# Layer norm and silu of a convolution in PSUM banks of their own, and silu's cast one tile later in ScalarE's order

## The chip, the cores and the metric

One core of a Trainium2 chip runs the kernel: TensorE (PE in the rows), VectorE (DVE), ScalarE (ACT), GpSimd (POOL), and SyncE (SP), which starts the loads and stores. The metric is the device time of one execution in microseconds, the median of the runs shown. Lower is better.

## The reference

A decoder layer on 512 tokens of width 1024, in float32. Two mixers work on the same normed input and are gated and added; an MLP with a squared ReLU follows. What matters here, cut down:

```python
u = rms_norm(x, norm_mix_g)
q, k, v, glu_in, gates = split(u @ w_in)
attn = sliding_window_attention(norm(q), norm(k), v, sinks, rel_bias) @ w_attn_o
a, gate = split(glu_in)
h = depthwise_conv(a * sigmoid(gate), w_dw, width=31) + b_dw
conv = silu(layer_norm(h, ln_g, ln_b)) @ w_conv_out
x = x + (sigmoid(gate_attn) * attn + sigmoid(gate_conv) * conv) @ w_out
x = x + square(relu(rms_norm(x, norm_mlp_g) @ w_ff1)) @ w_ff2
```

## The kernel before

**Tiling.** Activations stand transposed, 128 channels by 512 tokens to a tile; a projection to 1024 channels has eight such tiles. Every float32 product is made of three matmuls: each operand is split into a high part (rounded to fp32r, a cast on ScalarE) and a low part (the rest, a subtraction on GpSimd or VectorE), and high x high, high x low and low x high are added up in one PSUM bank. So a tile takes 8 x 3 = 24 matmuls of 512 columns.

**Stages.** First attention, the input projections and the 31 taps of the convolution (VectorE), side by side. Then the stage of the change: the attention output projection (`wo`, tiles ps_wo_0 to ps_wo_7), and beside it on the other engines the layer norm and silu of the eight convolution tiles; then the convolution output projection (`wc`, ps_wc), whose inputs are silu's high part sTh and low part sTl of all eight tiles; then w_out and the MLP in four parts, the second product of which keeps six banks in use at a time (ps_x, ps_y, ps_z, two each).

**Order.** Up to the end of `wc`, the order of the instructions on each engine is written out by hand: `at(position, function, arguments)` records an event, and the events are issued in the order of their positions (L992). One unit of position is six matmuls of a projection tile. Within an engine the order is strict; the engines wait for each other only through data and through buffers.

**Banks.** PSUM has eight banks. Two belong to the pool `aux`. The other six become the pool `psp` when attention closes (L830): one ring under the tag "mm". A tile asked for takes a bank of the ring, and if that bank's former tile still has readers, the first instruction that writes the new tile waits for them. In that ring stand the projection tiles, the mean (mu_ps), six squares (lsq) and eight silu values (y), in the order in which events ask for them.

**Layer norm.** `mean` (L854) makes the mean with two matmuls; `centre` (VectorE, L860) subtracts it; `square` (ScalarE, L868) squares, six of the tiles into PSUM; `square_sum` (VectorE, L876) adds them up in vsum; `var` (L880) sums over channels with sixteen small matmuls, takes 1/sigma on VectorE, and `spread` (L888) spreads it over the partitions with TensorE. Then per tile: `scale` (VectorE, L895), `silu_in` (ScalarE, L898: tanh into tz, then an affine y into PSUM), `silu` (VectorE, L905: y = (tz + 1) y), `silu_hi` (ScalarE, L909: the cast to sTh), `silu_lo` (VectorE, L912: sTl). On ScalarE stand between them the casts of the weight splits (L449), each followed by its low part on GpSimd (L452); SyncE's next load of weights waits for that low part. The evacuations of `wo` are on VectorE (L612), those of `wc` are three passes of VectorE and one of ScalarE (L614 to L619).

From w_out on, tiles are asked for in program order, again from `psp`.

Of the kernel before, what the change touches and what calls it, by code (L numbers as in the profile page):

```python
# [8 lines left out]
F32 = mybir.dt.float32  # L9
# [5 lines left out]
PSUM = bass.MemoryType.PSUM  # L15
DRAM = bass.MemoryType.DRAM

P = 128
S = 512
NT = 4  # L20
# [32 lines left out]
def tile_hybrid_block(  # L53
# [106 lines left out]
    def stationary_tiles(w, c0, n_tiles, name, lo_eng=None):  # L160

        for ch in range(n_tiles // 2):
            raw = wp.tile([P, KD, 256], F32, name=f"raw_{name}_{ch}", tag="raw", bufs=2)
            cols = slice(c0 + ch * 256, c0 + ch * 256 + 256)
            for kh in range(2):
                nc.sync.dma_start(
                    raw[:, 4 * kh:4 * kh + 4, :],
                    w[512 * kh:512 * kh + 512, cols].rearrange("(k p) c -> p k c", p=P),
                )
            for j in range(2):  # L170
                yield split(raw[:, :, j * P:(j + 1) * P], [P, KD, P], f"{name}_{ch}_{j}", lo_eng or ge)

    def moving_pieces(w, r0, nk, c0, width, name, lo_eng=None):

        kk = 1024 // width
        for ch in range(nk // (2 * kk)):
            raw = wp.tile([P, 2 * kk, width], F32, name=f"rawm_{name}_{ch}", tag="raw", bufs=2)
            for j in range(2):
                r = r0 + (ch * 2 + j) * kk * P
                nc.sync.dma_start(  # L180
                    raw[:, j * kk:(j + 1) * kk, :],
                    w[r:r + kk * P, c0:c0 + width].rearrange("(k p) c -> p k c", p=P),
                )
            for j in range(2):
                yield split(raw[:, j * kk:(j + 1) * kk, :], [P, kk, width], f"{name}_{ch}_{j}", lo_eng or ge)

    def mm_T(ps, wh, wl, ah, al, cols=slice(0, S), nk=KD):

        for k in range(nk):
            pe.matmul(ps, wh[:, k, :], ah[:, k, cols], start=(k == 0), stop=False)  # L190
            pe.matmul(ps, wh[:, k, :], al[:, k, cols], start=False, stop=False)  # L191
            pe.matmul(ps, wl[:, k, :], ah[:, k, cols], start=False, stop=(k == nk - 1))  # L192

    def mm_M(ps, ah, al, wh, wl, first, last):

        pe.matmul(ps, ah, wh, start=first, stop=False)  # L196
        pe.matmul(ps, ah, wl, start=False, stop=False)  # L197
        pe.matmul(ps, al, wh, start=False, stop=last)  # L198
# [144 lines left out]
    def at(pos, fn, *args):  # L343
        events.append((pos, len(events), fn, args))
# [109 lines left out]
    pool_of = {"mm": ps1}  # L454
# [178 lines left out]
    lnv = {}  # L633
# [168 lines left out]
    while any(left.values()):  # L802
# [3 lines left out]
        if live:  # L806
            ct = live[turn % len(live)]
# [19 lines left out]
    def close_attention():  # L827
        p1.close()
        pps.close()
        pool_of["mm"] = ctx.enter_context(tc.tile_pool(name="psp", bufs=6, space=PSUM, reuse_waits="tile"))  # L830
        lnv["pool"] = p2.enter_context(tc.tile_pool(name="ln", bufs=1, reuse_waits="tile"))
        aTh["t"] = lnv["pool"].tile([P, KD, S], F32R, name="aTh")
        lnv["sTh"] = lnv["pool"].tile([P, KD, S], F32R, name="sTh")
        lnv["sTl"] = lnv["pool"].tile([P, KD, S], F32R, name="sTl")
        lnv["vsum"] = [lnv["pool"].tile([P, S], F32, name=f"vsum{i}") for i in range(2)]
# [4 lines left out]
    def a_lo(g):  # L840
        if g == 0:
            aTh["l"] = keep.tile([P, KD, S], F32R, name="aTl", tag="act", bufs=2)
        ve.tensor_tensor(out=aTh["l"][:, 2 * g:2 * g + 2, :], in0=attnT[g],
                         in1=aTh["t"][:, 2 * g:2 * g + 2, :].bitcast(F32), op=ALU.subtract)

    at(END - 0.01, close_attention)
    for g in range(NG):
        at(END + 0.3 + g, a_hi, g)
        at(WO + 0.1 + 0.5 * g, a_lo, g)

    def lt(name):
        return lnv["pool"].tile([P, S], F32, name=name, tag="lt", bufs=4)
# [15 lines left out]
    def square(ct):  # L868
        vs = lnv["vsum"][ct % 2]
        if ct >= 6:  # L870
            se.activation(vs, cc[ct], AF.Square)
        else:
            sq = lnv["sq", ct] = pool_of["mm"].tile([P, S], F32, name=f"lsq_{ct}", tag="mm")
            se.activation(sq, cc[ct], AF.Square)

    def square_sum(ct):  # L876
# [20 lines left out]

    def silu_in(ct):  # L898
        tz = lt(f"tz_{ct}")
        y = pool_of["mm"].tile([P, S], F32, name=f"y_{ct}", tag="mm")  # L900
        lnv["y", ct] = (tz, y)
        se.activation(tz, cc[ct], AF.Tanh, scale=lnh[:, ct, 0:1], bias=lnh[:, ct, 1:2])
        se.activation(y, cc[ct], AF.Identity, scale=wcol[:, ct, CW + 1:CW + 2], bias=wcol[:, ct, CW + 2:CW + 3])
# [14 lines left out]
    for i, ct in enumerate((6, 7, 0, 1, 2, 3, 4, 5)):  # L918
        at(E + 1.3 + 0.5 * i, centre, ct)
        at(E + 1.7 + 0.5 * i, square, ct)  # L920
        if ct < 6:
            at(E + 2.8 + 0.5 * i, square_sum, ct)
    at(E + 8.5, var)
    at(E + 11.05, spread)
    for ct in range(KD):
        p = E + 11.1 + 1.35 * ct
        at(p, scale, ct)
        at(p + 0.5, silu_in, ct)
        at(p + 1.4, silu, ct)
        at(p + 1.7, silu_hi, ct)  # L930
        at(p + 2.75, silu_lo, ct)

    def merge_tiles():
        for n in "hl":
# [5 lines left out]
    with tc.manual_schedule(engines=START_ENGINES):  # L940
# [50 lines left out]
            pass  # L991
        for _, _, fn, args in sorted(events, key=lambda e: e[:2]):  # L992
            fn(*args)
    psp = pool_of["mm"]
    mTh, mTl = mT["h"], mT["l"]
    p2.close()
    gp.close()
# [20 lines left out]
    def mm_rows(accs, pieces, ah, al, kk):  # L1018

        n = len(pieces)  # L1020
        for i in range(n):
            for j in range(kk):
                for t in range(NT):
                    k = i * kk + j
                    mm_M(accs[t], ah(k, t), al(k, t), pieces[i][0][:, j, :], pieces[i][1][:, j, :], k == 0,
                         k == n * kk - 1)
# [3 lines left out]
    def residual(t, half, acc):  # L1030
        cols = slice(half * S, half * S + S)
        ve.tensor_tensor(out=x1[t][:, cols], in0=x1[t][:, cols], in1=acc, op=ALU.add)
        sq = row4k(f"fsq_{half}{t}")
        se.activation(sq[:, 0:S], x1[t][:, cols], AF.Square, accum_out=ssm[:, t, half:half + 1])

    def m_hi(k, t):
        return mTh[:, k, t * P:(t + 1) * P]

    def m_lo(k, t):
        return mTl[:, k, t * P:(t + 1) * P]  # L1040

    accs = [psp.tile([P, S], F32, name=f"ps_wo0_{t}", tag="mm") for t in range(NT)]
    mm_rows(accs, list(moving_pieces(w_out, 0, KD, 0, S, "wout0")), m_hi, m_lo, 2)
    for t in range(NT):
        residual(t, 0, accs[t])
# [11 lines left out]
    def x2_norm(t):  # L1057
        ms = sm.tile([P, 1], F32, name=f"ms_m{t}", tag="ms1")
        ve.tensor_tensor(out=ms, in0=ssm[:, t, 0:1], in1=ssm[:, t, 1:2], op=ALU.add)
        rs = rsqrt(mean_eps(ms, D, 1, f"m{t}"), 1, f"m{t}")  # L1060
        us[t] = row4k(f"u2_{t}")
        ve.scalar_tensor_tensor(out=us[t], in0=x1[t], scalar=rs, in1=gmlp, op0=ALU.mult, op1=ALU.mult)

    def x2_trans(t):
        transpose_split(aux, (us[t][:, 0:S], us[t][:, S:D]), x2Th, x2Tl, t, f"m{t}", "aux")

    for t in range(NT):
        acc = psp.tile([P, S], F32, name=f"ps_wo1_{t}", tag="mm")
        for k in range(KD):
            mm_M(acc, m_hi(k, t), m_lo(k, t), wout_h[k // 4][:, k % 4, :], wout_l[k // 4][:, k % 4, :],  # L1070
                 k == 0, k == KD - 1)
        residual(t, 1, acc)
        x2_norm(t)
        if t == 2:
            x2_trans(0)
# [31 lines left out]
    for part in range(PARTS):  # L1107
        tag = f"f{part}"
# [28 lines left out]

        early = []
        for m, (wh, wl) in enumerate(stationary_tiles(w_ff1, part * PT * P, PT, f"f1{part}", ve)):
            ps = psp.tile([P, S], F32, name=f"ps_f1{part}_{m}", tag="mm")  # L1140
            if part == 0 and m < EARLY:
                mm_T(ps[:, 0:256], wh, wl, x2Th, x2Tl, slice(0, 256))
                early.append((ps, wh, wl))
                if m < 2:
                    x2_trans(2 + m)
                if m == EARLY - 1:
                    for i, (ps_, wh_, wl_) in enumerate(early):
                        mm_T(ps_[:, 256:512], wh_, wl_, x2Th, x2Tl, slice(256, 512))
                        ff1_evac(ps_, i)
            else:  # L1150
                mm_T(ps, wh, wl, x2Th, x2Tl)
                ff1_evac(ps, m)
# [38 lines left out]
                    nc.sync.dma_start(out[n * P:(n + 1) * P, cols], x1[n][:, cols])  # L1191

        def two_banks(name):
            return [psp.tile([P, S], F32, name=f"ps_{name}{t}_{part}", tag="mm") for t in range(2)]

        def S_(i):
            return lambda t: a_of(aS, i, t)

        b11, b12, b22 = load(0, 0), load(0, 1), load(1, 1)
        X, Y = two_banks("x"), two_banks("y")  # L1200
        product(lambda t: a_of(aE, None, t), pieces_of(b11, f"b11_{part}"), X, True, True)
        add(0, 0, X, False)
# [58 lines left out]
```

## Time and profile before

| | us |
|---|---|
| median of 3 runs | 790.45 (789.98 to 791.97) |
| the profiled execution | 791.01 |
| its span, first to last instruction | 789.1 |
| TensorE busy in it | 775.8 |
| VectorE, ScalarE, GpSimd busy | 562.3, 404.8, 254.4 |

All times of rows are microseconds from the start of the span. A row of the timeline has the start, the duration, the engine, the line, the operation, what is written and from what, the shape, the count, and in brackets how long the engine stood idle before it and whom it waited for. Matmuls are pipelined: the distance from start to start counts, not the duration of one. [...]

### The profile page before, as it was taken

How to read it: one execution, taken by the hardware profiler on the slowest of the kernel's cores; microseconds unless marked ns; L12 is line 12 of the kernel's file. 1: busy time of each engine (PE TensorE's matmuls, PEld its weight loads, DVE VectorE, ACT ScalarE, POOL GpSimd, SP SyncE). 2: the span in 40 equal slices, each digit the busy share in tenths (PEclk: the TensorE clock that was granted, in tenths of full speed). 3: DMA queues.
4: the chain of work that ended last, by engine and by line, in shares of the span. 5: the costliest groups of instructions: out<-in, count | busy, mean ns of one | idle time of the engine just before them, and what ended most of it. 6: DMA issues, size and time to landing. Idle time of an engine off the chain costs nothing.

```text
span 789.1 us, 10436 instructions
## 1 busy us (share of the span) xinstructions
PE 775.8 (98%) x3960; PEld 658.2 (83%) x3960; DVE 562.3 (71%) x949; ACT 404.8 (51%) x683; POOL 254.4 (32%) x189
## 2 busy tenths in 40 slices
PE   8999999999999999998999999999999999999998
PEld 7989988898888888786888898888888888888886
DVE  5467978998888878966330886886678756875683
ACT  6445467676576655446233346443554365435640
POOL 4444978958565665423445000000000000000000
PEclk9999999999999999999999999999999999999999
DMA  7441041214141133422335344143224233331102
GB/s 255 139 154 54 3 158 54 92 43 134 53 135 54 56 105 102 166 69 91 107 107 155 100 149 157 54 159 103 68 97 148 69 105 108 107 106 54 36 19 106
DMA packets 64807, 79.56 MB, mean 101 GB/s; under 512 B 2980, under 2 KB 52180, under 8 KB 64758
## 3 DMA queue, kind: packets, MB, share of 16 engines
q1 hardware_dynamic: 64758, 78.91, 30.0%
q8 instruction: 31, 0.51, 0.3%
q14 instruction: 18, 0.15, 0.1%
HBM read 76.78 MB, written 2.12 MB: 100 GB/s over the span
## 4 chain that ended last, share of the span: by engine, by line
PE 89%; ACT 4%; DVE 3%; POOL 2%; DMA 1%; issue 1%; SPq 0%; DVEq 0%; ACTq 0%; POOLq 0%
PE ps_f L191 7%; PE ps_f L192 7%; PE ps_f L190 7%; PE ps_x L1181 4%; PE ps_x L1182 4%; PE ps_x L1179 4%; PE ps_ta L484 2%; PE ps_ta L486 2%; PE ps_g L484 2%; PE ps_ta L485 2%; PE ps_wo L198 2%; PE ps_wo L197 2%; PE ps_y L1181 2%; PE ps_y L1182 2%; PE ps_y L1179 2%; PE ps_wo L196 2%
## 5 line engine op out<-in xcount | busy, mean ns | idle before, releaser
L782 DVE SCALAR_TENSOR_TENSOR cv<-h,wcol,cv 128x512 f32<-128x512 f32 x208 | 147.5, 747 | 0.5
L191 PE MATMUL ps_f<-x2Tl,wh_f 128*128 128x512 f32 (+1 forms) x280 | 104.1, 372 | 0.1
L190 PE MATMUL ps_f<-x2Th,wh_f 128*128 128x512 f32 (+1 forms) x280 | 103.6, 371 | 0.2 <-ACT x2Th L208 0.2
L192 PE MATMUL ps_f<-x2Th,wl_f 128*128 128x512 f32 (+1 forms) x280 | 103.8, 371 | 0.0
L157 DVE TENSOR_TENSOR wl_f<-raw_f,wh_f 128x1024 fp32r<-128x1024 f32 x32 | 39.2, 1224 | 59.8 <-ACT wh_f L156 58.8
L156 ACT CAST wh_f<-raw_f 128x1024 fp32r<-128x1024 f32 x32 | 33.6, 1055 | 55.4 <-PE ps_f L191 36.9
L190 PEld LDWEIGHTS ps_f<-x2Th,wh_f 128*128 128x128 f32 x280 | 52.6, 188 | 9.6 <-ACT x2Th L208 0.5
L191 PEld LDWEIGHTS ps_f<-x2Tl,wh_f 128*128 128x128 f32 x280 | 52.7, 188 | 9.3 <-DVE x2Tl L209 0.3
L192 PEld LDWEIGHTS ps_f<-x2Th,wl_f 128*128 128x128 f32 x280 | 52.7, 188 | 9.0
L1102 ACT CAST wh_b<-b 128x1024 fp32r<-128x1024 f32 x24 | 25.3, 1056 | 40.5 <-PE ps_y L1182 13.1
L1089 DVE TENSOR_TENSOR wl_b<-b,wh_b 128x1024 fp32r<-128x1024 f32 x24 | 29.3, 1223 | 22.2 <-ACT wh_b L1102 22.2
L1102 ACT CAST wh_t<-t 128x1024 fp32r<-128x1024 f32 x24 | 24.9, 1054 | 35.5 <-DVE t L1089 15.6
L691 ACT ACTIVATE s<-s,negm 128x257 f32<-128x257 f32 (+1 forms) x64 | 30.4, 478 | 16.3 <-DVE negm L683 16.3
L196 PE MATMUL ps_q<-wh_q,uTh 128*128 128x256 f32 x128 | 36.6, 286 | 0.0
L198 PE MATMUL ps_q<-wh_q,uTl 128*128 128x256 f32 x128 | 36.2, 283 | 0.0
L197 PE MATMUL ps_q<-wl_q,uTh 128*128 128x256 f32 x128 | 36.2, 283 | 0.0
L715 DVE TENSOR_TENSOR pTl<-ptp,pTh 128x512 fp32r<-128x512 f32 x28 | 19.3, 691 | 23.4 <-ACT pTh L711 23.4
L774 POOL TENSOR_TENSOR side<-side,tap 128x512 f32<-128x512 f32 x24 | 31.2, 1299 | 13.6 <-ACT tap L773 13.6
L1089 DVE TENSOR_TENSOR wl_t<-t,wh_t 128x1024 fp32r<-128x1024 f32 x24 | 29.0, 1221 | 5.9 <-ACT wh_t L1102 5.4
L700 POOL TENSOR_TENSOR s<-s,r 128x1024 f32<-128x1024 f32 (+1 forms) x16 | 26.9, 1682 | 14.7 <-DVE r L695 14.7
L683 DVE CUSTOM_DVE_ANT_0 s<-sp,bias,rb_sink 128x256 f32<-128x256 f32 (+1 forms) x64 | 26.2, 446 | 5.1 <-PE sp L676 4.9
L452 POOL TENSOR_TENSOR wl_wo<-raw_wo,wh_wo 128x1024 fp32r<-128x1024 f32 x8 | 19.6, 2462 | 29.3 <-ACT wh_wo L449 29.3
(298 smaller groups left out, 2305.2 us busy)
## 6 DMA issues: line engine op xcount, KB each, us to landing
raw_f<-in_w_ff_dram SPq DMA_DIRECT2D x32, 512.0 KB, 4.3
b<-in_w_ff_dram SPq DMA_DIRECT2D x32, 512.0 KB, 4.1
x<-in_x_dram SPq DMA_DIRECT2D x8, 512.0 KB, 4.7
raw_g<-in_w_in_dram SPq DMA_DIRECT2D x8, 512.0 KB, 4.1
raw_a<-in_w_in_dram SPq DMA_DIRECT2D x8, 512.0 KB, 3.5
raw_q<-in_w_in_dram SPq DMA_DIRECT2D x8, 512.0 KB, 4.4
raw_ta<-in_w_in_dram SPq DMA_DIRECT2D x8, 512.0 KB, 4.5
raw_tc<-in_w_in_dram SPq DMA_DIRECT2D x8, 512.0 KB, 3.6
```

Source lines behind the costliest of these rows:

```text
L190: pe.matmul(ps, wh[:, k, :], ah[:, k, cols], start=(k == 0), stop=False)
L191: pe.matmul(ps, wh[:, k, :], al[:, k, cols], start=False, stop=False)
L192: pe.matmul(ps, wl[:, k, :], ah[:, k, cols], start=False, stop=(k == nk - 1))
L196: pe.matmul(ps, ah, wh, start=first, stop=False)
L197: pe.matmul(ps, ah, wl, start=False, stop=False)
L198: pe.matmul(ps, al, wh, start=False, stop=last)
L782: ve.scalar_tensor_tensor(out=cps[ct], in0=src, scalar=w, in1=cps[ct], op0=ALU.mult, op1=ALU.add)
L1089: ve.tensor_tensor(out=out, in0=a, in1=b, op=ALU.subtract)
L1102: se.copy(wh, half)
L1179: pe.matmul(banks[t], ah, wh[:, j, :], start=(first and h + j == 0), stop=False, skip_group_check=True)
L1181: pe.matmul(banks[t], ah, wl[:, j, :], start=False, stop=False, skip_group_check=True)
L1182: pe.matmul(banks[t], al, wh[:, j, :], start=False, stop=(last and h + j == 2), skip_group_check=True)
```

## The change

The ring of six under one tag becomes two rings of three in one pool, "ln" and "mm"; a first tile without a use gives "ln" the first three banks. The squares and the silu values come from "ln"; the projection tiles and the mean stay in "mm". After the hand-ordered part, `bank` asks for tiles in turn, three from "ln" and three from "mm". In the order, `silu_hi` of a tile moves from 1.7 to 2.4 units behind its `scale`, which on ScalarE puts it behind `silu_in` of the next tile, and `silu_lo` moves from 2.75 to 3.0, which on VectorE puts it behind `silu` of the next tile.

```diff
     def close_attention():
-        pool_of["mm"] = ctx.enter_context(tc.tile_pool(name="psp", bufs=6, space=PSUM, reuse_waits="tile"))
+        pool_of["mm"] = ctx.enter_context(tc.tile_pool(name="ps3", bufs=3, space=PSUM, reuse_waits="tile"))
+        pool_of["mm"].tile([P, S], F32, name="first", tag="ln")
...
     def square(ct):
-            sq = lnv["sq", ct] = pool_of["mm"].tile([P, S], F32, name=f"lsq_{ct}", tag="mm")
+            sq = lnv["sq", ct] = pool_of["mm"].tile([P, S], F32, name=f"lsq_{ct}", tag="ln")
...
     def silu_in(ct):
-        y = pool_of["mm"].tile([P, S], F32, name=f"y_{ct}", tag="mm")
+        y = pool_of["mm"].tile([P, S], F32, name=f"y_{ct}", tag="ln")
...
         at(p, scale, ct)
         at(p + 0.5, silu_in, ct)
         at(p + 1.4, silu, ct)
-        at(p + 1.7, silu_hi, ct)
-        at(p + 2.75, silu_lo, ct)
+        at(p + 2.4, silu_hi, ct)
+        at(p + 3.0, silu_lo, ct)
...
-    psp = pool_of["mm"]
+    banks = ["ln", "ln", "ln", "mm", "mm", "mm"]
+
+    def bank(name):
+
+        banks.append(banks.pop(0))
+        return pool_of["mm"].tile([P, S], F32, name=name, tag=banks[-1])
...
-    accs = [psp.tile([P, S], F32, name=f"ps_wo0_{t}", tag="mm") for t in range(NT)]
+    accs = [bank(f"ps_wo0_{t}") for t in range(NT)]
...
-            ps = psp.tile([P, S], F32, name=f"ps_f1{part}_{m}", tag="mm")
+            ps = bank(f"ps_f1{part}_{m}")
...
-            return [psp.tile([P, S], F32, name=f"ps_{name}{t}_{part}", tag="mm") for t in range(2)]
+            return [bank(f"ps_{name}{t}_{part}") for t in range(2)]
```

## Rows read from the trace of the kernel before

**Rows 1.** The page's busy table: busy us, share of the span, instructions.

```profile
PE 775.8 (98%) x3960; PEld 658.2 (83%) x3960; DVE 562.3 (71%) x949; ACT 404.8 (51%) x683; POOL 254.4 (32%) x189
```

**Rows 2.** TensorE's waits, 290 to 420 and behind: us in total, times, longest.

```profile
PE ps_wc L484 <- ACT sTh L910: 2.2, 1, 2.2
PE ps_wo L484 <- DVE vsum L878: 1.6, 1, 1.6
...
PE ps_f L190 <- ACT x2Th L208: 0.2, 1, 0.2
```

**Rows 3.** Stages: length, busy us (count) of five engines, clock, DMA share, GB/s.

```profile
330.20:331.90 1.70, 0.13 (x2) 0.07 (x1) 1.70 (x4) 1.02 (x2) 0.00 (x0) 1.00 0.00 0
...
366.90:369.20 2.30, 0.08 (x2) 0.02 (x1) 0.74 (x2) 1.54 (x4) 1.92 (x1) 1.00 0.00 0
369.20:372.60 3.40, 3.40 (x7) 2.42 (x8) 2.64 (x4) 0.86 (x1) 2.38 (x1) 0.50 0.79 256
```

**Rows 4.** Timeline of TensorE around the first pause.

```profile
329.87 0.39 PE L486 MATMUL ps_wo<-aTh,wl_wo 128*128 128x512 f32 x1
331.83 0.50 PE L484 MATMUL ps_wo<-aTh,wh_wo 128*128 128x512 f32 x1 [1.57 <-DVE vsum L878]
...
332.63 0.40 PE L484 MATMUL ps_wo<-aTh,wh_wo 128*128 128x512 f32 x1
```

**Rows 5.** Timeline of TensorE around the second pause.

```profile
366.57 0.39 PE L486 MATMUL ps_wc<-sTh,wl_wc 128*128 128x512 f32 x1
369.18 0.79 PE L484 MATMUL ps_wc<-sTh,wh_wc 128*128 128x512 f32 x1 [2.22 <-ACT sTh L910]
...
372.87 0.40 PE L486 MATMUL ps_wc<-sTh,wl_wc 128*128 128x512 f32 x1
```

**Rows 6.** Timeline of VectorE: the last square sums, the end of 1/sigma.

```profile
334.09 1.87 DVE L878 TENSOR_TENSOR vsum<-vsum,lsq 128x512 f32<-128x512 f32 x3
...
342.77 0.17 DVE L116 SCALAR_TENSOR_TENSOR y_ln<-a_ln,y_ln 128x4 f32<-128x4 f32 x1
```

**Rows 7.** Timeline of TensorE: variance, spread, first matmul of wc.

```profile
337.40 1.84 PE L884 MATMUL var_ps<-ones,vsum 128*128 128x1 f32 x16
...
343.33 0.94 PE L892 MATMUL rv_ps<-ident,y_ln 128*128 128x128 f32 x7
...
361.97 0.39 PE L484 MATMUL ps_wc<-sTh,wh_wc 128*128 128x512 f32 x1
```

**Rows 8.** Timeline of ScalarE: first tanh, a whole tile of silu, last cast.

```profile
345.14 0.82 ACT L902 ACTIVATE tz<-h,eps_ln 128x512 f32<-128x512 f32 x1 [6.68 <-DVE h L896]
...
350.72 0.81 ACT L902 ACTIVATE tz<-h,eps_ln 128x512 f32<-128x512 f32 x1
...
352.96 0.60 ACT L910 ACTIVATE sTh<-y 128x512 fp32r<-128x512 f32 x1 [0.76 <-DVE y L907]
353.45 0.81 ACT L902 ACTIVATE tz<-h,eps_ln 128x512 f32<-128x512 f32 x1
...
368.53 0.60 ACT L910 ACTIVATE sTh<-y 128x512 fp32r<-128x512 f32 x1 [0.76 <-DVE y L907]
```

**Rows 9.** ScalarE's waits, 320 to 420.

```profile
ACT sTh L910 <- DVE y L907: 5.3, 7, 0.8
```

**Rows 10.** The silu stage: busy us of PE, PEld, DVE, ACT, POOL.

```profile
345.00:369.20 24.20, 21.98 (x98) 17.63 (x96) 16.29 (x27) 18.72 (x28) 7.17 (x3) 1.00 0.14 44
```

**Rows 11.** Timeline of VectorE: the last low part of silu.

```profile
369.16 0.69 DVE L913 SCALAR_TENSOR_TENSOR sTl<-y,sTh 128x512 fp32r<-128x512 f32 x1 [0.66 <-ACT sTh L910]
```

**Rows 12.** Timeline of VectorE: first and last pass over a wc tile.

```profile
410.03 0.70 DVE L615 SCALAR_TENSOR_TENSOR ps_wc<-tc,ps_wc 128x512 f32<-128x512 f32 x1 [2.66 <-PE ps_wc L486]
...
412.12 0.69 DVE L618 SCALAR_TENSOR_TENSOR mTl<-ps_wc,mTh 128x512 fp32r<-128x512 f32 x1 [0.67 <-ACT mTh L617]
```

**Rows 13.** Timelines of VectorE and TensorE where an MLP part begins.

```profile
539.83 1.34 DVE L1189 TENSOR_TENSOR x<-x,ps_x 128x512 f32<-128x512 f32 x2
...
540.28 0.39 PE L190 MATMUL ps_f<-x2Th,wh_f 128*128 128x512 f32 x1
```

More of the change, by code (lines that the diff above doesn't have):

```diff
@@ L1067, in tile_hybrid_block @@
     for t in range(NT):
-        acc = psp.tile([P, S], F32, name=f"ps_wo1_{t}", tag="mm")
+        acc = bank(f"ps_wo1_{t}")
         for k in range(KD):
```

## The prediction

> **What bounds the kernel now.** Four views, in this order. The busy table of the page says that TensorE works nearly all the time [rows 1], so a change is worth what it takes out of TensorE's pauses, plus what it does to TensorE's clock. The table of waits, asked for TensorE, then lists the pauses: in the stage that the change touches there are two, and after 420 us there is none above 0.2 us [rows 2]. One is an output projection tile (ps_wo) that waits for a square sum of the layer norm on VectorE, the other a convolution projection tile (ps_wc) that waits for a silu cast (sTh) on ScalarE. The stage table shows what TensorE's clock did around them: granted 1.00 across the first pause, 1.00 in the second, and 0.50 in the 3.4 us behind the second, where only seven matmuls ran [rows 3]. [...] Third, the timeline gives their size. Undisturbed, one of these matmuls follows the other every 0.23 us (21 of ps_wc from 361.97 to 366.57, 20 steps [rows 5, 7]). From 329.87 to 332.63 lie four steps, 0.92 us at that pace, and they took 2.76: the first pause costs 1.84 us [rows 4]. From 366.57 to 372.87 lie nine steps, 2.07 us at pace, and they took 6.30: the second costs 4.23 us, clock included [rows 5]. Together 6.07 us is what there is to win. Last, ScalarE's and VectorE's timelines say what keeps those two results late; they are read below.
>
> **The banks.** No instruction is added or removed: the same tiles go to other banks. Before, one ring of six holds projection tiles, mean, squares and silu values in the order in which they are asked for. ps_wo_3 is asked for at position 172.0, when in the written order the only banks given back and not taken again are those behind the first square sums; it gets the one that held lsq_1, and has to wait for VectorE's second square sum, though the projection tiles before it were long done. That is the pause of [rows 4]. After, ps_wo_3 finds in the ring "mm" the bank of ps_wo_1, which VectorE empties even before the mean is taken. So the wait goes. What is late next: the variance matmuls stand on TensorE right behind ps_wo_3, and they need the last square sum. TensorE would come to them at 337.40 - 1.84 = 335.56 [rows 7]; VectorE's last three square sums run from 334.09 for 1.87 us, to 335.96 [rows 6], and nothing in their order changes. So 0.40 us is given back as a new wait at var_ps, with a restart like that of [rows 4] (three steps in 0.80 instead of 0.69) about 0.5. I bound it by 0.4 below and by 0.84 above (the whole 0.4 once more, should the weight load, here the square sum itself, lie bare). Net: 1.84 - 0.5 = **1.3 us**, between 1.0 and 1.45. Queued behind that wait are ps_wo_4 and then the spreading of 1/sigma (rv_ps). The spread was reached at 343.33 with its input finished at 342.94 [rows 6, 7]; both hang on var_ps, so both move by 1.3 and the relation stays.
>
> The ring of three for the layer norm adds waits in name. lsq_3 to lsq_5 take the banks of lsq_0 to lsq_2, so each waits for the square sum three before it; on VectorE that sum stands ahead of the very centring whose result the square needs anyway, so I cost it at nothing. Were that cover gone, one VectorE pass each, 0.6 us. A silu value y_n waits for the low part (silu_lo) of tile n-3; on VectorE this stands before the scaling of tile n-1, for which tanh n-1 has already waited on ScalarE. Nothing again. Behind a blocked y_n would queue the cast of n-1 and a weight split, and TensorE would feel it only once the slack worked out below is used up. The three "mm" banks serve the projections: a tile of wc holds its bank for its matmuls and about 3 us of evacuation (410.03 to 412.81 [rows 12]), and its bank is asked for again two tiles, 2 x 24 x 0.23 = 11 us, after its end. Covered. If not, see rival (d).
>
> **The cast one tile later.** Eight tiles of silu go through ScalarE as tanh, affine (y), cast (sTh). Between y and cast VectorE multiplies, and ScalarE, being in order, stands still: 0.76 us in the tile from 350.72 to 353.45, 2.73 us long [rows 8]; seven such waits, 5.3 us [rows 9]. From the first tanh to the end of the last cast it takes 345.14 to 369.13, that is 23.99 us [rows 8], and that end releases TensorE at 369.18 [rows 5]. After, the cast of n-1 stands behind tanh and y of n, so VectorE's multiply runs beside them. The waits go, 5.3; seven casts no longer begin after a drained instruction (about 0.07 each, 0.5); the last tile still waits, partly beside the cast of tile 6, about 0.2. Chain: 24.0 - 5.3 - 0.5 + 0.2 = 18.4 us. The three weight splits between stay; the one for wo_7 now even comes before the cast of tile 0. Their loads on SyncE's queue wait for GpSimd's low parts, which come earlier with them, never later; no DMA is moved past another. Is VectorE fast enough? In that stage it was busy 16.3 of 24.2 us, ScalarE 18.7 [rows 10], so ScalarE stays the bound, barely. I laid both queues out anew, instruction by instruction, with the starts and durations of this trace; the same method gives the old order its last cast at 368.48, against 368.53 measured [rows 8].
>
> So the last cast ends at 345.14 - 1.3 + 18.4 = 362.2, and its low part about 0.75 later, at 363.0 (before: 369.85 [rows 11]). TensorE wants them at 366.57 + 0.23 - 1.3 = 365.5. There are 3 us to spare, so the whole second pause goes with its slow clock: **4.2 us**. Bounds: all of it while the chain is shortened by more than 2.8 us (369.85 - 1.3 against 365.7, where the low part is wanted), nothing if it isn't shortened at all.
>
> **The banks of the rest.** From the output projection on, bank() deals the six out in turn, the same turn as one ring in this part, except that a bank can only be had from its own half. The place to look at is where an MLP part begins: its first tiles may get a bank of ps_x, which VectorE empties last. Before, the next part's matmuls begin at 540.28, and the two additions run from 539.83 for 1.34 us, to 541.17 [rows 13]. If the bank given back first is taken first, as with ps_wo_3, only the second tile of a part (5.4 us later) meets ps_x, and this costs nothing; if banks are dealt in fixed turn, it is up to 541.17 - 540.28 = 0.9 us, three times, 2.7. I take nothing, since [rows 4] fits the first kind alone: a fixed turn would have given ps_wo_3 the bank of the mean.
>
> **Sum.** 1.3 + 4.2 = 5.5 us. The profiled execution took 791.01 us (span 789.1, 1.9 around it), 0.56 above the median of 790.45; a difference carries over: 790.45 - 5.5 = **784.9**. By its bounds (1.0 to 1.45, and 3.9 to 4.3) and the scatter of the runs shown, 783.7 to 786.3.
>
> **Rivals.** (a) *The reorder moves the wait instead of removing it*: VectorE, with 16.3 us of work, falls behind, and ScalarE waits for scalings as it did for the multiply. For it: the loads of the two are close [rows 10]. Against: it must eat nearly 3 of the 5.6 us. If it eats all, 790.45 - 1.3 = 789.1. (b) *The first pause turns wholly into the wait for the variance*, three square sums late by 0.6 each in their narrower ring: 790.45 - 4.2 = 786.2. Against it, the order on VectorE. (c) *The MLP parts wait for ps_x*, 2.7 us: 787.6. (d) *Slower*: three banks are too few for the projections, and TensorE stops at every wc tile for the evacuation of the one before. The price is 3.0 us for each of eight tiles [rows 12], 24 us: 790.45 - 5.5 + 24 = 809; it decides against the change from 0.7 us a tile on, and needs an evacuation that ends 11 us after its tile instead of 3. The tightest bank I find is wo_6's, emptied in VectorE's queue at about 360 and wanted by wc_1 at 361.97 - 1.3 + 5.5 = 366.2 [rows 7], 6 us to spare. [...] (e) *The change does not do what it says*: ps_wo_3 still meets a late bank, that of the mean, whose last reader follows the second square sum by three passes of 0.6 us on VectorE [rows 6]. The first gain becomes a loss of 1.8, 790.45 - 4.2 + 1.8 = 788.1, and with a slow restart such as the second pause had (4.2 less its 2.4 us of idleness, 1.8) 789.9.
>
> **How the numbers follow.** The forecast 0.78; (a) 0.04; (b) 0.06; (c) 0.04; (d) 0.05; (e) 0.03. The forecast's own range is where most of the chance lies; I reach up to (b) and (c), and leave 0.2 below for a chain that shrinks the stage's other waits too: 783.5 to 787.6, without (a), (d) and (e). About 0.3%, 2.4 us, can be told from no change here, so faster means under 788.1: the forecast, (b) and (c), 0.88, of which scatter may take 0.01; (a), (e) and that, 0.08; slower, (d), 0.05.
>
> **What would show it.** TensorE's waits should lose ps_wo <- vsum and ps_wc <- sTh, and gain one at var_ps <- vsum of about 0.4 us; rv_ps should begin near 342.0, ps_wc near 360.7, and no stage behind should have a clock under 1.00. ScalarE's wait sTh <- y should fall from 5.3 us to under 0.5, with the last cast ending near 362.2. In the MLP no wait of ps_f for ps_x. The forecast is wrong if wc's tiles wait for a bank or a weight, or if the last cast ends after 365.5.

## The result, and the profile of the changed kernel

The changed kernel took 785.88 us (median of four runs, 785.06 to 787.25) against 791.21 us for the kernel before (789.98 to 792.00): a ratio of 0.9929, with a 95% interval of [0.9913, 0.9946], or 5.6 us less by the ratio (4.3 to 6.9); the two medians lie 5.3 apart. Run again later it took 787.51 (786.68 to 787.75, six runs) against 791.94, a ratio of 0.9945 [0.9931, 0.9959], 4.4 us less (3.2 to 5.5). The forecast was 784.9.

The totals of two single executions can mislead. The profiled execution of the changed kernel took 787.25 us with a span of 785.5, only 3.6 less than the span of before, because it lost 2.2 us at its very beginning, in work that the change does not touch. In both fences below the columns are start, duration, engine, line, operation, tiles, shape and count, with the idle time ahead of it and its releaser in brackets. TensorE's timeline from 0 to 12 us, before and then after:

```profile
1.46 7.10 PE L222 MATMUL warm<-ident 128*128 128x128 f32 x36 [1.46 <-POOL eps_ln L121]
10.11 1.09 PE L206 MATMUL tp_u<-ident,u 128*128 128x128 f32 x8 [1.54 <-DVE u L295]
```

```profile
1.46 5.73 PE L222 MATMUL warm<-ident 128*128 128x128 f32 x36 [1.46 <-POOL eps_ln L121]
10.19 1.09 PE L206 MATMUL tp_u<-ident,u 128*128 128x128 f32 x8 [3.00 <-DVE u L295]
```

These are 18 warming matmuls of the kernel (`warm`), each of which the profile lists as two entries. The same 36 entries took 5.73 us instead of 7.10, because the step from one to the next fell from 0.21 us to 0.11 at 4.5 us and not at 7.4. TensorE then had nothing to do for 3.00 us instead of 1.54, and in the stretch that follows its granted clock, a share of its full speed as in [rows 3], was 0.53, where it was 1.00 before:

```profile
11.00:18.00 7.00, 6.62 (x31) 6.09 (x30) 5.94 (x9) 4.67 (x9) 5.69 (x2) 0.53 0.68 253
```

So from here on I measure the **stage**: from the first matmul of ps_wo_2 (the tile ahead of the first pause) to the first matmul of the output projection w_out. It was 86.08 us before (323.75 to 409.83) and 80.19 after (325.97 to 406.16), 5.89 less. What lies behind it, up to the end, took 379.29 and 379.30 us: nothing was won or lost there.

TensorE's waits after, which answer [rows 2] (us in total, times, longest):

```profile
PE tp_u L206 <- DVE u L295: 3.0, 1, 3.0
...
PE ps_f L190 <- ACT x2Th L208: 0.2, 1, 0.2
PE var_ps L885 <- DVE vsum L879: 0.2, 1, 0.2
```

Both waits of the stage are gone, and one at var_ps has come, as forecast. In the stage table (columns as in [rows 3]) the clock is 1.00 throughout, TensorE is busy without a gap in the silu stage, and VectorE and ScalarE are busy for 18.5 and 19.2 of its 24.2 us (before 16.3 and 18.7 [rows 10]), since work that came behind silu now falls into the same stretch:

```profile
339.90:344.00 4.10, 4.10 (x19) 3.41 (x19) 3.48 (x13) 0.00 (x0) 1.38 (x1) 1.00 0.75 251
345.00:369.20 24.20, 24.20 (x108) 20.01 (x108) 18.53 (x30) 19.15 (x28) 9.65 (x4) 1.00 0.26 87
```

TensorE's timeline after, which answers [rows 5, 7]: the variance, its next tile, the spread of 1/sigma, and wc's first matmul and the first that needs the last cast. The sixteen entries at var_ps are eight matmuls of the kernel, two to each of four token tiles; the first two entries are one matmul, over the sum of the even tiles.

```profile
337.77 0.28 PE L885 MATMUL var_ps<-ones,vsum 128*128 128x1 f32 x2
338.25 1.72 PE L885 MATMUL var_ps<-ones,vsum 128*128 128x1 f32 x14 [0.21 <-DVE vsum L879]
339.84 0.48 PE L484 MATMUL ps_wo<-aTh,wh_wo 128*128 128x512 f32 x1
...
344.03 1.05 PE L893 MATMUL rv_ps<-ident,y_ln 128*128 128x128 f32 x8
...
362.64 0.39 PE L484 MATMUL ps_wc<-sTh,wh_wc 128*128 128x512 f32 x1
...
367.40 0.39 PE L484 MATMUL ps_wc<-sTh,wh_wc 128*128 128x512 f32 x1
```

ScalarE's timeline after, which answers [rows 8]: the first tanh, then tanh and affine of one tile and the cast of the tile before it, and the last cast; and its wait for VectorE's multiply, which answers [rows 9].

```profile
345.85 0.82 ACT L903 ACTIVATE tz<-h,eps_ln 128x512 f32<-128x512 f32 x1 [7.01 <-DVE h L897]
...
350.12 0.80 ACT L903 ACTIVATE tz<-h,eps_ln 128x512 f32<-128x512 f32 x1
350.82 0.76 ACT L904 ACTIVATE y<-h,wcol 128x512 f32<-128x512 f32 x1
351.53 0.57 ACT L911 ACTIVATE sTh<-y 128x512 fp32r<-128x512 f32 x1
352.00 0.80 ACT L903 ACTIVATE tz<-h,eps_ln 128x512 f32<-128x512 f32 x1
...
363.71 0.60 ACT L911 ACTIVATE sTh<-y 128x512 fp32r<-128x512 f32 x1 [0.24 <-DVE y L908]
```

```profile
ACT sTh L911 <- DVE y L908: 0.2, 1, 0.2
```

A tile now takes 1.88 us on ScalarE (350.12 to 352.00) where it took 2.73 [rows 8]. The last cast ends at 364.31 and TensorE comes for it at 367.40.

### The profile page after: what moved, and what is told of

It is laid out like the page before. It is cut to its first block, busy times and chain, and to the rows that moved or that the text cites. A ratio compares the mean times of both kernels' runs of the same rounds, so it can differ in the third digit from the quotient of the medians.

```text
span 785.5 us, 10448 instructions
## 1 busy us (share of the span) xinstructions
PE 774.8 (99%) x3960; PEld 658.8 (84%) x3960; DVE 561.5 (71%) x949; ACT 404.2 (51%) x683; POOL 254.3 (32%) x189
## 4 chain that ended last, share of the span: by engine, by line
PE 92%; DVE 3%; POOL 2%; ACT 1%; DMA 1%; issue 1%; SPq 0%; DVEq 0%; POOLq 0%; ACTq 0%
PE ps_f L191 7%; PE ps_f L192 7%; PE ps_f L190 7%; PE ps_x L1189 4%; PE ps_x L1186 4%; PE ps_x L1188 4%; PE ps_ta L484 2%; PE ps_ta L486 2%; PE ps_g L484 2%; PE ps_ta L485 2%; PE ps_wo L198 2%; PE ps_wo L196 2%; PE ps_wc L486 2%; PE ps_wc L484 2%; PE ps_y L1189 2%; PE ps_y L1186 2%
## 5 line engine op out<-in xcount | busy, mean ns | idle before, releaser
L1096 DVE TENSOR_TENSOR aSl<-ss,aSh 128x1024 fp32r<-128x1024 f32 x16 | 19.6, 1225 | 13.2 <-ACT aSh L1122 13.2
```

The costliest lines, as they stand in the source:

```text
L1096: ve.tensor_tensor(out=out, in0=a, in1=b, op=ALU.subtract)
```

## The experiments

There were two questions. Does each half of the change do what the prediction says, with the price it says? And, once the first profiles had come, why was the same kernel's stage 80.19 us in one execution and 81.82 in another?

This table gathers one profiled execution of each kernel. "Var" says whether TensorE waits at var_ps, and "var to rv" is the time from its first matmul there to the first of rv_ps (18 matmuls of ps_wo lie between). "Chain" is ScalarE's from the first tanh to the end of the last cast, "wc wait" the longest wait of a ps_wc tile.

| kernel | stage | start of stage | var | var to rv | chain | wc wait |
|---|---|---|---|---|---|---|
| before | 86.08 | 323.75 | none | 5.93 | 23.99 | 2.2 |
| after | 80.19 | 325.97 | 0.2 | 6.26 | 18.46 | none |
| e1_banks_only | 86.26 | 324.74 | 0.2 | 7.88 | 23.99 | 2.2 |
| e2_order_only | 81.71 | 324.99 | none | 5.92 | 18.46 | none |
| e3_cast_twice | 84.09 | 325.88 | 0.2 | 6.26 | 23.14 | 1.0 |
| e5_lo_not_moved | 81.78 | 323.60 | 0.2 | 7.83 | 20.04 | none |
| e0_after_again | 81.82 | 324.57 | 0.2 | 7.89 | 18.47 | none |
| e4_cast_twice_even | 80.20 | 325.01 | 0.2 | 6.26 | 20.61 | none |
| e6_var_later | 79.85 | 325.96 | none | 5.93 | 18.46 | none |
| e7_warm28 | 80.19 | 323.71 | 0.2 | 6.26 | 18.47 | none |
| e8_both | 79.85 | 323.74 | none | 5.92 | 18.46 | none |
| e9_before_warm28 | 86.46 | 323.81 | none | 5.93 | 23.99 | 2.2 |
| e10_banks_only_warm28 | 86.29 | 323.91 | 0.2 | 7.89 | 23.99 | 2.2 |
| e11_before_warm28_again | 86.49 | 323.86 | none | 5.92 | 23.98 | 2.2 |

**Each half alone.** First the banks without the new order. Edit, against the changed kernel:

```
-        at(p + 2.4, silu_hi, ct)
-        at(p + 3.0, silu_lo, ct)
+        at(p + 1.7, silu_hi, ct)
+        at(p + 2.75, silu_lo, ct)
```

> The change with silu_hi and silu_lo put back to 1.7 and 2.75: the banks alone. The stage is counted from the first matmul of ps_wo_2 to the first matmul of w_out, so that the start of the kernel plays no part: 86.1 us before, 80.2 after the change. Theory (two separate pauses, one for each part of the change): the first pause goes and 0.4 comes back at var_ps, the second pause and its slow clock stay whole: stage 86.1 - 1.5 = 84.6 us, time 1.5 us under before, ScalarE's wait sTh <- y back at 5.3 us. Rival (the first pause is only passed on): the silu chain hangs on VectorE's square sums and ends as late as before, the second pause grows by what the first gave, stage 86.1, time as before.

Measured: 791.64 us against 791.09, ratio 1.0001 [0.9990, 1.0012], and a stage of 86.26. The banks alone bought nothing. The wait of ps_wo is gone; the other two are those of before:

```profile
PE ps_wc L484 <- ACT sTh L911: 2.2, 1, 2.2
...
ACT sTh L911 <- DVE y L908: 5.3, 7, 0.8
```

The stage comes out as the rival said, that the gain is passed on to the second pause, but not by its way: ScalarE's chain is as long as before. The time went right behind var_ps, where 7.88 us passed up to rv_ps instead of 6.26, with the clock at 0.57 (columns as in [rows 3]):

```profile
339.74:343.74 4.00, 4.00 (x13) 3.11 (x12) 2.57 (x12) 0.00 (x0) 0.31 (x1) 0.57 0.55 192
```

That had no place in the forecast.

Then the order without the banks: the kernel before, with the two times of silu_hi and silu_lo at 2.4 and 3.0 (the edit above read backwards, in the kernel before).

> The kernel before with silu_hi at 2.4 and silu_lo at 3.0: the order alone, one ring of six. Theory: ps_wo_3 still takes the bank of lsq_1 and waits 1.6 us for the second square sum; the second pause goes with its slow restart, 4.3 us: stage 86.1 - 4.3 = 81.8 us, time 4.3 us under before. Rival (silu needs banks of its own for the new order, since a y now lives a tile longer): ScalarE or TensorE meets new bank waits in the silu stage and the gain is under 2 us, stage above 84.

Measured: 787.24 against 791.09, ratio 0.9953 [0.9939, 0.9967], 3.7 us less; a stage of 81.71, 4.37 below that of before. TensorE still waits for the square sum, and ScalarE hardly for the multiply:

```profile
PE ps_wo L484 <- DVE vsum L878: 1.6, 1, 1.6
...
ACT sTh L910 <- DVE y L907: 0.2, 1, 0.2
```

So the second pause goes by the order alone, with the time that was forecast for it (4.2).

**How much is spare behind the new order.** In the changed kernel each cast is done twice:

```
         se.activation(lnv["sTh"][:, ct, :], lnv["y", ct][1], AF.Copy, scale=0.5)
+        se.activation(lnv["sTh"][:, ct, :], lnv["y", ct][1], AF.Copy, scale=0.5)
```

> The change, with every cast to sTh done twice: eight more ScalarE instructions of 0.48 us in the chain, the result the same. Theory (ScalarE sets the chain, with 3.1 us to spare after the change): the last cast ends 3.6 us later against TensorE, the spare time is used up by about half a microsecond, and the low part comes 0.7 behind it: a pause of about 1.0 us returns at the last channel tile of the first ps_wc, at the high clock; stage 80.2 + 1.0 = 81.2 us. Rival (VectorE sets the chain, ScalarE has room): the extra casts disappear, stage 80.2. Rival (no spare time at all): stage 80.2 + 3.8 = 84.

Measured: 789.13 against 791.09, ratio 0.9982 [0.9970, 0.9994], and a stage of 84.09, much above what was expected. Two things were wrong in my number. A second cast cost about 0.6 us instead of 0.48: in all eight tiles the second write of the same tile started only 0.03 us after the first had ended (ScalarE's timeline), where tanh, affine and cast start 0.05 to 0.10 us before the instruction ahead has ended:

```profile
349.55 0.58 ACT L911 ACTIVATE sTh<-y 128x512 fp32r<-128x512 f32 x1
350.17 0.60 ACT L912 ACTIVATE sTh<-y 128x512 fp32r<-128x512 f32 x1
```

The chain grew by 4.68 us, past the 3.1 that were spare, and a pause of 1.03 us came of it, with two more waits of 0.23 and 0.15 us, for low parts, close behind. TensorE's clock fell there, to 0.52 in the 3.4 us behind, as it did to 0.50 behind the 2.2 us pause of before [rows 3] (TensorE's timeline and the stretch behind, columns as in [rows 3]):

```profile
367.83 0.49 PE L484 MATMUL ps_wc<-sTh,wh_wc 128*128 128x512 f32 x1 [1.03 <-ACT sTh L912]
...
369.60:373.00 3.40, 3.32 (x8) 2.65 (x9) 2.01 (x4) 0.84 (x3) 2.37 (x1) 0.52 0.78 271
```

From 366.42 to 373.21 lie 13 steps, 2.95 us at pace, and they took 6.79: 3.84 us, nearly all of the 3.90 by which the stage is longer. With the second cast for tiles 0, 2, 4 and 6 only:

```
+        if ct % 2 == 0:
+            se.activation(lnv["sTh"][:, ct, :], lnv["y", ct][1], AF.Copy, scale=0.5)
```

> The change, with the casts of tiles 0, 2, 4 and 6 done twice: four more ScalarE instructions, 1.9 us in the chain, the result the same. Theory (3.1 us to spare): hidden whole, no wait of ps_wc for sTh, stage 80.2 us. Rival (the chain ends just in time, without room): stage 82.

Measured: 786.58 against 791.94, ratio 0.9933 [0.9915, 0.9951]; the chain is 2.15 us longer, TensorE waits for no cast, and the stage is 80.20, that of the changed kernel to 0.01. So about 2 us more on ScalarE are hidden and 4.7 are not: the 3 us that the prediction had to spare stand between them.

The other moved step is the low part. Here the cast is late as in the change, and silu_lo stays where it was:

```
-        at(p + 3.0, silu_lo, ct)
+        at(p + 2.75, silu_lo, ct)
```

> The change with silu_lo left at 2.75, so that on VectorE the low part of a tile stands ahead of the multiply of the next tile. Theory: VectorE's multiply now waits behind a low part that waits for the cast; ScalarE's wait sTh <- y comes back in part (about 1.5 us in the eight tiles), the last cast ends some 1.4 us later, and the 3.1 us of spare time hide it: stage 80.2 us. Rival (the move of the low part carries the gain, because the two engines lock step without it): sTh <- y back near 5 us, a pause of over 1 us at ps_wc, stage above 81.5.

Measured: 786.65 against 791.09, ratio 0.9939 [0.9923, 0.9955]. VectorE's low part, waiting for a cast, now stands ahead of a multiply that ScalarE needs: ScalarE waits 1.4 us, once, and the chain grows by 1.58, all of it hidden. That the stage is 81.78 is the clock behind var_ps again (7.83 us up to rv_ps, and 0.61 from 338.60 to 342.60). So moving the low part only widens the margin.

**Where the clock goes behind var_ps.** The changed kernel, unaltered, run again:

> The change itself once more, for its time and its first 20 us. [...] Theory (the start is a lottery of its own, in both kernels): stage 80.2 us again whatever the start does, and the time between 785.0 and 787.3 by the clock of the start alone. Rival (the change makes the start slower, by another order of its loads): every run shows the slow start.

Its times stand in the section on the result. Its profiled execution has the same waits, but a stage of 81.82, not the 80.2 that I expected. All six runs have a mean clock under 1.000, as the rival expects, by which the change slows the start. But two of the first four runs of the same kernel have 1.000 (785.18 and 785.06 us; the other two, 787.25 and 786.57, have 0.996 and 0.998), and in e5, which is the same kernel up to the stage, the stage began at 323.60. TensorE's timeline there, and the stretch behind the variance:

```profile
336.37 0.28 PE L885 MATMUL var_ps<-ones,vsum 128*128 128x1 f32 x2
336.86 1.72 PE L885 MATMUL var_ps<-ones,vsum 128*128 128x1 f32 x14 [0.21 <-DVE vsum L879]
...
339.17 0.63 PE L486 MATMUL ps_wo<-aTh,wl_wo 128*128 128x512 f32 x1
339.59 0.63 PE L484 MATMUL ps_wo<-aTh,wh_wo 128*128 128x512 f32 x1
...
344.26 0.94 PE L893 MATMUL rv_ps<-ident,y_ln 128*128 128x128 f32 x7
```

```profile
338.40:341.80 3.40, 3.40 (x11) 2.71 (x11) 2.81 (x13) 0.00 (x0) 1.47 (x1) 0.55 0.92 304
```

Wait and variance are those of the first profile to 0.02 us, and then one ps_wo matmul follows another every 0.42 us instead of every 0.23, at a granted clock of 0.55. Eight such steps cost 8 x 0.2 = 1.6 us, which is the whole difference of the two stages (1.63).

If the wait at var_ps is what does it, taking its cause away must end it. In the next kernel the variance, and with it the spread and silu, come one place later in the written order, so that TensorE does six matmuls of ps_wo more, 1.36 us, before it needs the square sums:

```
-    at(E + 8.5, var)
-    at(E + 11.05, spread)
+    at(E + 9.5, var)
+    at(E + 12.05, spread)
...
-        p = E + 11.1 + 1.35 * ct
+        p = E + 12.1 + 1.35 * ct
```

> The change with var, spread and all of scale and silu one unit (six matmuls) later in the written order. Theory: TensorE does six matmuls of ps_wo_4 while VectorE ends the last square sum, so the 0.4 us at var_ps that the banks gave back goes; the silu chain starts 1.0 us later against TensorE and its spare time shrinks from 3.1 to about 2, still hidden: stage 79.8 us, 0.4 us under the change. Rival (the chain has no such room, or the spread now makes TensorE wait): stage 80.2 or more.

Measured: 784.67 against 791.94, ratio 0.9912 [0.9897, 0.9927]. No wait at var_ps, the clock at 1.00 behind it, a stage of 79.85. The 0.34 us below 80.19 are about the wait itself. Four of its six runs lie between 784.60 and 784.71; the others, 785.50 and 786.89, have a mean clock of 0.997 and 0.996, and the profiled one of these had lost 2.2 us at the start (325.96).

To take that start out too, ten more warming matmuls, in the changed kernel and in the one with the later variance:

```
-WARM = 18
+WARM = 28
```

> The change with 28 instead of 18 matmuls ahead of the first real work (WARM). [...] Theory: the longer row reaches to the first transposes at 10 us in every run, the clock stays at 1.00 and the slow group of times goes: all runs between 784.9 and 785.6, mean clock 1.000; stage 80.2. Rival (the slow start has another cause, the loads): the two groups stay. [...]

> The change with var and all behind it one unit later (as in the run with var later) and 28 matmuls at the start. [...] Theory (the 0.4 us wait at var_ps, in front of sixteen matmuls of one column, makes the clock fall in a part of the executions): without the wait it never falls, and with the longer start the other slow group goes too: one group of times, 784.2 to 785.0, stage 79.8. Rival (the one-column matmuls alone let the clock fall): two groups 1.6 us apart, as with 28 matmuls and var in its old place (785.0 and 787.0).

Measured: the changed kernel with it 785.90 against 791.94, ratio 0.9927 [0.9911, 0.9943]; its runs fall into 784.98, 785.02, 785.07 and 786.73, 786.99, 787.24, so the two groups that I expected to become one are still there. Both edits: 784.80 (784.70 to 784.91, five runs) against 791.96, ratio 0.9909 [0.9896, 0.9923], 7.2 us less than before. The first edit leaves two kinds of executions, the second added to it leaves one, within 0.21 us. Its TensorE around the variance, and that stretch:

```profile
336.90 1.84 PE L885 MATMUL var_ps<-ones,vsum 128*128 128x1 f32 x16
338.60 0.49 PE L484 MATMUL ps_wo<-aTh,wh_wo 128*128 128x512 f32 x1
...
337.00:341.00 4.00, 4.00 (x27) 3.56 (x26) 1.85 (x12) 0.00 (x0) 2.04 (x1) 1.00 0.74 256
```

The same sixteen entries of one-column matmuls, without a wait among them, take 1.70 us to the next tile, and the clock stays at 1.00. It is 1.1 us at the median below the changed kernel with the longer warming and 2.7 below it as it is (787.51 in e0), without their scatter. At the median it does not differ from e6 (784.67), but e6 has runs up to 786.89.

**The same start for the kernels compared.** Last, the warming was put under the kernel before and under the banks alone (edits as above), the former a second time, since its first profile showed a longer stage than that of before.

> The kernel before with 28 instead of 18 matmuls at the start, nothing else. Theory (the start is a lottery of both kernels, and before has no wait at var_ps): the times draw together at the fast end of the kernel before, 789.5 to 790.5, median 0.5 to 1.5 under before; stage 86.1. Rival (the groups of times come from the rest of the kernel): the spread of before, 789.6 to 792.9, stays.

> The banks alone (silu_hi and silu_lo at their old places) with 28 matmuls at the start. Theory (the banks win 1.5 us and the clock behind var_ps takes 1.6 back in a part of the executions): two groups of times, one 1.5 us under the kernel before with the same start, about 788.3, one at its level or slightly over, about 790.0. Rival (the banks alone are worth nothing whatever the clock does): one group at the level of the kernel before with the same start.

> The kernel before with 28 matmuls at the start once more, for a second profile. Its times lay in two groups, about 789.9 and 791.5, though the start was the same. Theory (the 2.2 us pause at ps_wc lets the clock fall only in a part of the executions): a profile of the fast group shows a stage of about 84.4 us with the clock at 1.00 behind the pause, one of the slow group 86.1 to 86.5 with 0.50 for some 3.4 us. Rival (the groups come from elsewhere): stage 86.1 to 86.5 in both.

Measured: before with the longer warming 791.36 against 791.96, ratio 0.9994 [0.9983, 1.0005], and again 791.44, ratio 0.9985 [0.9970, 1.0000]; the banks alone with it 789.61, ratio 0.9969 [0.9957, 0.9980]. In all five profiles with the longer warming the stage starts between 323.71 and 323.91, where it started between 323.60 and 325.97 with the shorter. I expected the runs of before to draw together as well. They did not, and each run's span and mean granted clock say why (spans in us, number of runs):

| kernel, all with 28 warming matmuls | clock 1.000 | clock 0.997 to 0.998 | clock under 0.997 |
|---|---|---|---|
| before (e9, e11) | 787.9 to 788.7 (8) | 789.4 to 790.4 (12) | none |
| banks alone (e10) | 786.4 to 786.6 (4) | 787.3 to 788.3 (5) | 789.0 to 789.5 (2) |
| the change (e7) | 783.2 to 783.3 (3) | 784.9 to 785.5 (3) | none |
| the change, variance later (e8) | 782.9 to 783.1 (5) | none | none |

By my estimate 3.4 us at a clock of 0.50, as in [rows 3], lower the mean of a run of some 788 us by 0.002. So the columns count the falls, nearly: e9's and e11's profiles have the same clocks around the second pause, 0.79 and 0.81 in the 3.4 us behind it and 0.86 in the next 7.4, and a mean of 0.998 and 0.997. Before has one place for them, the second pause; the banks alone have two, the second pause and var_ps (their profiled execution, of 791.41 us, had both); the change has one, var_ps; the last kernel has none. Along the first column, where no clock fell, the banks are worth 788.1 - 786.5 = 1.6 us and the order 786.5 - 783.2 = 3.3, each a difference of means.

## Why the prediction was right, and where it was not

**The first pause** went as forecast. The wait of ps_wo for the square sum is gone, and the variance came next: from its first matmul to the next tile lie 2.07 us (337.77 to 339.84) where it is 1.70 without a wait (e8). So 1.84 was won and 0.37 given back, 1.47 net, a hair above the bounds; the forecast was 0.5 and 1.3. The longest wait listed is 0.21, not 0.4, because the first two of the sixteen entries read a square sum that was ready.

**The step that failed** is the term for that wait. I gave it a restart "like that of [rows 4]" and an upper end of 0.84. Its length was sized well, its price was not: in four of the eight profiled executions that have it (e0, e1, e5, e10), the clock fell right behind it, to 0.55, 0.57, 0.61 and 0.57 in stretches of 3.4 to 4 us, and it cost 0.37 + 1.62, about 2.0 us. Without the wait, but with the same matmuls, it was 1.00 there in all six (before, e2, e6, e8, e9, e11). It does not go by the start alone: the stages with the fall began between 323.60 and 324.74, and those without between 323.71 and 325.97. So "no stage behind should have a clock under 1.00" held in the profile that came first and not in e0, and it explains all of e1: the banks alone won 1.47 and paid 1.62. What went into the forecast was my reading that the pause of 1.57 us left the clock alone, at 1.00 [rows 3, 4]. Behind that pause, between tiles of 512 columns, it stayed at 1.00 in all four profiles that have it (before, e2, e9, e11). I carried that over to a wait with one-column matmuls on both sides, and there it held in four profiles of eight.

**The cast one tile later** went as forecast almost to the digit. With the later start of 2.22 us taken off, in brackets the forecast: rv_ps began at 341.81 (342.0), ps_wc at 360.42 (360.7), the last cast ended at 362.09 (362.2), and TensorE wanted it at 365.18 (365.5). The chain was 18.46 (18.4), the wait sTh <- y 0.2 (under 0.5), and 3.1 us were spare (3). Laying ScalarE's and VectorE's queues out anew, with the durations of the trace of before, was thus worth the pains. The experiments bear it out from both sides: 2.15 us more of casts are hidden (e4), 4.68 are not (e3).

**The second pause** was worth 4.37 in e2's stage, where 4.2 was forecast. But that price holds the fall of the clock, which I took for certain. It fell in all five profiles that have the pause (0.50 in before, 0.64 from 371 to 375 us in e1, and in e9, e10 and e11 0.79, 0.58 and 0.81 in the 3.4 us behind it), though in e9 and e11 it came later than in [rows 3], at 371.2 and 371.3. In e11 (columns as there):

```profile
366.60:369.20 2.60, 0.51 (x2) 0.08 (x1) 0.70 (x1) 1.84 (x4) 2.35 (x1) 1.00 0.00 0
369.20:372.60 3.40, 3.04 (x10) 2.22 (x11) 2.68 (x4) 1.32 (x3) 2.31 (x1) 0.81 0.72 239
```

Until then a matmul followed another every 0.23 to 0.24 us once the two waits were over (e9's clock was 0.97 from 369.20 to 371.30), and the pause had cost 3.0 us already. In e9's timeline of TensorE, from 366.63 to 371.00 lie six steps, 1.36 us at pace, and they took 4.37:

```profile
366.63 0.40 PE L486 MATMUL ps_wc<-sTh,wl_wc 128*128 128x512 f32 x1
369.24 0.50 PE L484 MATMUL ps_wc<-sTh,wh_wc 128*128 128x512 f32 x1 [2.22 <-ACT sTh L910]
369.97 0.50 PE L485 MATMUL ps_wc<-sTl,wh_wc 128*128 128x512 f32 x1 [0.22 <-DVE sTl L913]
...
371.00 0.46 PE L486 MATMUL ps_wc<-sTh,wl_wc 128*128 128x512 f32 x1
```

The second matmul behind the pause needs VectorE's low part of the same tile, which follows the cast, and comes 0.5 us late by that. In before this step takes the same 0.73 us, but the profile shows no wait there. So the prediction's split of 4.2 into 2.4 of idleness and 1.8 of slow restart gave the clock too much: the wait for the low part was in it, and the clock's own share in before is about 1.2 (4.23 less 3.0).

In eight of the twenty runs of e9 and e11 the mean clock says that it did not fall, and there the order is worth 3.3. So the whole gain is had in a pair of executions with the fall before and none after, as the first two profiles are: 5.89 us of stage, 1.47 and some 4.4. Over all runs with the same start (e9 and e11, e7) the mean spans, 789.0 and 784.2 us, differ by 4.8.

**The MLP's banks** cost nothing, as taken. Where a part begins (VectorE's and TensorE's timelines, which answer [rows 13]), the first tile starts while the additions that empty ps_x still run:

```profile
536.17 1.34 DVE L1196 TENSOR_TENSOR x<-x,ps_x 128x512 f32<-128x512 f32 x2
...
536.63 0.39 PE L190 MATMUL ps_f<-x2Th,wh_f 128*128 128x512 f32 x1
```

**The rivals.** (a), that VectorE would fall behind, is out: the chain is 18.46 us. (b) named the right place, var_ps, and the wrong cause: the square sums were not later than before, and what the place cost beyond 0.37 was the clock; in the executions with the fall the total comes to 786.7 to 787.2 (e7), a little over (b)'s 786.2, all the same. (c) is out by the row above. (d) is out at the wc tiles, where TensorE ran without a gap at a clock of 1.00 (busy for 33.2 of the 33.2 us from 372.80 to 406.00). (e) is out: ps_wo waits for nothing.

The range held because the two mistakes were small beside it: the wait's price was 0.4 or 2.0 where 0.5 stood, and the start, which neither the forecast nor the change touches, moved single runs by up to 2.2 us. Some of that is luck. The median of four runs, 785.88, lies well inside; that of the six runs of e0, 787.51, lies 0.1 under the upper end, and two of those runs lie above it. Counted as gains, 5.5 us was forecast, and 5.6 and 4.4 came. The narrower range of the sum, 783.7 to 786.3, did not hold in e0, and the bounds of 3.9 to 4.3 for the second pause, from which it comes, are worked out nowhere in the prediction.

## What to carry to other kernels

When a wait on the critical engine is removed, ask what that engine meets next and price that wait by what its clock does behind it, not by its length: here 0.2 us among one-column matmuls cost as much, in half of the profiled executions (about 2.0 us in four of eight), as the removed pause had (1.84), and one reordering by a single place made it go. On an engine that works in order, a step that needs another engine's answer belongs behind the next tile's independent work (ScalarE's waits for the multiply fell from 5.3 to 0.2 us); laying both queues out with the durations of the trace gave the chain's new length to a tenth of a microsecond (18.4 for 18.46). And compare kernels by a stage that begins and ends with the same instructions, and by runs with the same mean clock, before a microsecond of a total is believed.

## What the runs showed of the hardware that was not expected

- **The same program's clock falls in some executions and not in others.** Behind the wait of 0.2 us at var_ps in 4 of 8 profiles (0.55 to 0.61 in the next 3.4 to 4 us, and 1.00 in the other four); behind the pause of 2.2 us in 5 of 5 (0.50 in before), but by the mean clock in about 12 of 20 runs; behind a pause of 1.03 us, with 0.23 and 0.15 more, in the one profile that has it (e3, 0.52); behind the pause of 1.57 us in 0 of 4 (1.00). So length alone does not decide. What does was not settled; no run changes the narrow matmuls beside the short wait.
- **The pause of 2.2 us costs more than its length even where the mean clock reads 1.000**: 3.3 to 3.4 us of span (788.1 to 784.7 for e2, 786.5 to 783.2 for e10 and e7), where the next matmul came 2.4 us late by [rows 5]. The wait for the low part and the steps behind it bring that to the 3.0 that e9 and e11 had lost before their clock fell. None of the executions without a fall was profiled, and the last 0.3 to 0.4 stay open.
- **With 18 warming matmuls the start differed from one execution to the next.** The stage began anywhere from 323.60 to 325.97. Where the entries' step fell to 0.11 us early, at 4.5 us in the changed kernel's profile, the warming ended early and left a longer idle time behind it, 3.00 us; the clock then read 0.53 from 11 to 18 us. In the seven profiles with 1.9 to 3.1 us idle there the stage began at 324.57 to 325.97, in the two with 1.5 and 1.6 (before, e5) at 323.75 and 323.60. Over the first 20 us the clock was 0.91 in e2, one of the seven, and 1.00 in before. The mean clock of the runs of before goes down to 0.994 with 18 and not under 0.997 with 28. With 28 the stage began from 323.71 to 323.91 in five of five profiles.
- **A small VectorE instruction ended with a GpSimd split.** One pass over 128x4 integers (L111) took 1.09 us in the changed kernel, 1.48 before, and 0.17 in e6 and e8. In the changed kernel's trace it ends when GpSimd's split ends, 341.30 and 341.28, and in before and e9 it ends 0.02 and 0.03 us behind that split as well (340.95 and 340.93, 341.02 and 340.99):

```profile
338.91 2.37 POOL L452 TENSOR_TENSOR wl_wo<-raw_wo,wh_wo 128x1024 fp32r<-128x1024 f32 x1 [0.21 <-ACT wh_wo L449]
...
340.21 1.09 DVE L111 TENSOR_SCALAR y_ln<-ms_ln 128x4 int32<-128x4 int32 x1
```

  In e6 it began at 341.20, when the split (to 341.26) was all but over, and it took 0.17 us. In e8 the split ended at 339.04 and the pass, begun at 338.97, took 0.17 us too. Why the two end together was not settled. Nobody waited for it here, since the spread came later.
